# Two-layer hybrid encoder: PSUM banks divided 4 + 2 + 2, third branch's halves interleaved, one address residue for all matmul operands

## The chip, the cores and the metric

One core of a Trainium2 chip. The metric is the device time of one launch in microseconds (us); lower is better. TensorE multiplies, ScalarE (ACT) and VectorE (DVE) and GpSimd (POOL) do the elementwise work, SyncE (SP) issues the transfers.

## The reference

Input x is 256 tokens of 1024 channels, fp32. Two layers, each of three residual steps:

```
x = x + 0.5 * (silu(g) * u) @ w_ffn1_out          # g, u = split(rmsnorm(x) @ w_ffn1_in), 2816 wide each
h = rmsnorm(x); all of q, k, v and the three gates come from one product h @ w_in
a = softmax(rotary(norm(q)) @ rotary(norm(k))) @ v     # 8 heads on 2 key heads
b = softmax(q @ k + bias, window 128, with a sink) @ v # 8 heads on 2 key heads
c = norm((softmax1 - lambda * softmax2) @ v)           # 4 heads, 128 wide
m = sum over i in (a, b, c) of sigmoid(gate_i) * (i @ w_branch[i])   # 512 -> 1024 each
x = x + m @ w_out
x = x + 0.5 * swiglu(rmsnorm(x))                  # ffn2
```

At the end a last rmsnorm. All of it is in fp32.

## The kernel before

Activations stand feature-major: a tile is 128 channels by 256 tokens. A fp32 product is made of three fast ones. Every weight tile (1 MB) is loaded by SP into raw, rounded on ScalarE into hi (L302), and the rest, raw - hi, is made on VectorE as lo (L303); every activation is kept as such a pair too (xgh and xgl, hh and hl, ych and ycl, mh and ml). The helper mm3 issues for one 128x128 block hi with xh (L319), hi with xl (L320), lo with xh (L321), 256 columns each, into the same PSUM bank. hi and lo are split two tiles ahead of use, in three buffers each (pools whi and wlo); split allocates 32 elements more than a tile holds, and for the last FFN's output weights puts the data 16 elements in (L295 to L297). Ahead of everything three pools hold a pad of 16 elements (L112).

PSUM has eight banks of 128 x 512 fp32: four in pool acc under the tag bank (scores sc, transposed probabilities pt, yt, the output accumulators facc of an FFN and wacc of the mixer), one in acc under the tag o (value products o and oc, sums stps), three in wk (gate and up products gu, projections fm, values vps, branch products br). A bank is handed out in rotation and its first writer waits for the last reader of what it held before.

An FFN (ffn, L407) goes over 11 pairs of weight tiles: gate product, up product, then gr = silu on VectorE, ScalarE and POOL, hid = up * gr, the pair hh and hl, and the output product of the previous pair into facc. The last FFN makes its output token-major, with the hidden activations as the stationary operand and hi and lo moving.

The mixer (L618) makes keys, the first queries and values; then a generator (rest) yields projections and branch products in a fixed order (ORDER), and between yields step() takes the next piece of attention from a plan: scores, softmax, transposition, value product (pv, L593), and pair_out (L598 to L602), which reads the bank o and adds the halves into y. branch (L828) makes the products of the first two branches: per half n of the output two wk banks, 48 products; gated (L812) multiplies them with the gates (L817 for the first branch, L820 with an add on POOL, L821, for others). In the first half the k = 3 products come last, since the last y is made late. branch_c (L850) does the third branch: the first half in wk, and behind the sigmoid of its gate (L865) the second half in two banks of acc, three k steps of both first, then the k = 3 products. For the third branch gated also makes the pair mh (L824, ScalarE) and ml (L825, VectorE), four quarters in all, which the output projection takes one after the other, with four accumulators wacc from acc.

The order on TensorE is that of the program; ScalarE and VectorE are ordered by the scheduler for most of it.

Of the kernel before, what the change touches and what calls it, by code (L numbers as in the profile page):

```python
# [17 lines left out]
P = 128  # L18
# [52 lines left out]
def encoder(ctx: ExitStack, tc: tile.TileContext, a, rope, onehot, out):  # L71
# [12 lines left out]
    wk = ctx.enter_context(tc.tile_pool(name="wk", bufs=3, space=bass.MemoryType.PSUM))  # L84
# [17 lines left out]
    def bank_o(name):  # L102

        return acc.tile([P, 2, S], F32, tag="o", name=name, bufs=1)
# [7 lines left out]
    for pool in (p1, pv_, py):  # L112
        pool.tile([P, 16], F32, tag="pad", name="pad", bufs=1)
# [161 lines left out]
    last = {i for i, (_, shape) in enumerate(specs) if shape[0] == 2 and i >= len(specs) - 3 * NPAIR}  # L275
# [15 lines left out]
    def split(n, eng=None):  # L291

        _, shape = specs[len(parts)]
        raw = raws[len(parts)]

        n_el, off = shape[0] * shape[1], 16 if len(parts) in last else 0
        hi, lo = (pool.tile([P, n_el + 32], F32R, tag=t, name=t)[:, off:off + n_el].rearrange("p (a b) -> p a b", a=shape[0]) for pool, t in ((whi, "hi"), (wlo, "lo")))  # L297
        parts.append((hi, lo))
        n = shape[0] // n
        for i in range(0, shape[0], n):  # L300
            h = slice(i, i + n)
            nc.scalar.copy(out=hi[:, h], in_=raw[:, h])  # L302
            (eng or nc.vector).tensor_sub(lo[:, h], raw[:, h], f(hi[:, h]))  # L303
            yield
# [107 lines left out]
    def ffn(gnext, final=False):  # L412
# [60 lines left out]

        pend = None
        for j in range(NPAIR):
            pss = []
            for half in range(2):
                w = weights()
                ps = bank(wk, "gu")
                if j == 0 and half == 0:  # L480
                    project_first(ps, w)
                    stats_tok()
                else:
                    project(ps, w, 0)
                    if j == 0:
                        stats_bcast()
                    project(ps, w, 1)
                pss.append(ps)
            Rb = bc(state["R"], 2)
            gr = t2("gr")  # L490
            nc.vector.tensor_mul(gr, pss[0], Rb)
            nc.scalar.activation(out=gr, in_=gr, func=AF.Silu)  # L492
            nc.gpsimd.tensor_mul(gr, gr, Rb)  # L493
            hid = t2("hid")
            nc.vector.tensor_mul(hid, pss[1], gr)
            hh, hl = t2("hh", F32R), t2("hl", F32R)
            nc.scalar.copy(out=hh, in_=hid)  # L497
            nc.gpsimd.tensor_sub(hl, hid, f(hh))  # L498
            if pend:
                outp(*pend)  # L500
            pend = (j, hh, hl)
            if final and 2 <= j < 4:
                back(j - 2)
            if j == len(late):
                late.append(load_late(j))
# [107 lines left out]
    def mixer(l):  # L613
# [192 lines left out]
        def products(pss, w, y, ks, started):  # L806
            for mp in range(2):
                for t in range(2):
                    for k in ks:
                        mm3(pss[mp][:, t, :], w, k, cs(2 * mp + t), y[0][:, k, :], y[1][:, k, :], False, k == 3, start=(not started and k == 0 and t == 0))  # L810

        def gated(i, n, pss):  # L812
            for mp in range(2):
                m = 4 * n + 2 * mp
                ms, g = (T["gate", b][:, m:m + 2, :] for b in (0, i))
                if i == 0:
                    nc.vector.tensor_mul(ms, pss[mp], g)  # L817
                else:
                    tmp = t2("tmp")
                    nc.vector.tensor_mul(tmp, pss[mp], g)  # L820
                    nc.gpsimd.tensor_add(ms, ms, tmp)  # L821
                if i == 2:
                    mh, ml = t2("mh", F32R), t2("ml", F32R)
                    nc.scalar.copy(out=mh, in_=ms)  # L824
                    nc.vector.tensor_sub(ml, ms, f(mh))  # L825
                    merged.append((mh, ml))

        def branch(i, y, steps):  # L828
# [3 lines left out]
            for n in range(2):  # L832
                w = weights()
                pss = [bank(wk, "br") for _ in range(2)]
                if n == 0:
                    products(pss, w, y, range(3), False)
                    products(pss, w, y, (3,), True)
                else:
                    products(pss, w, y, range(4), False)
                gated(i, n, pss)  # L840
                for _ in range(2):
                    yield

        def branch_c(y, steps):
            while done[0] < steps:
                step()
            w0 = weights()
            ps0 = [bank(wk, "br") for _ in range(2)]
            products(ps0, w0, y, range(3), False)
# [4 lines left out]
            ps1 = [bank(acc, "br") for _ in range(2)]  # L854
            products(ps1, w1, y, range(3), False)
            products(ps0, w0, y, (3,), True)
            gated(2, 0, ps0)
            yield
            products(ps1, w1, y, (3,), True)
            gated(2, 1, ps1)  # L860
# [23 lines left out]
        ps_k = bank(wk, "fm")  # L884
# [26 lines left out]
        vps = [bank(wk, "vps") for _ in range(2)]  # L911
# [137 lines left out]
```

## Time and profile before

| | |
|---|---|
| median of 3 runs | 1228.72 us (1228.0 to 1229.53) |
| profiled execution | 1229.28 us |
| its span | 1227.2 us |
| mean granted TensorE clock | 0.988 |
| TensorE, weight loads, VectorE, ScalarE, POOL busy | 1185.0, 1160.7, 815.9, 677.5, 273.9 us |
| read from HBM | 215.59 MB |

The span runs from the first to the last instruction in the profile. Times in the rows below are microseconds from its start. PE is TensorE, PEld its weight loads, which overlap with products; a product's duration includes its way through the array, so the time from the start of one to the start of the next tells what it costs.

### The profile page before, as it was taken

The numbers are of one execution on the slowest core, as the hardware profiler recorded it, in microseconds if no ns is written. First come the engines' busy times: TensorE is split into PE (matmuls) and PEld (weight loads), VectorE is DVE, ScalarE is ACT, GpSimd is POOL, SyncE is SP. The second block draws the span as 40 slices with busy tenths as digits, with TensorE's granted clock in tenths as the row PEclk, the third lists the DMA queues.
The fourth block names the chain that finished last, engine by engine and source line by source line (L and its number), as shares of the span: only waits on it lengthen the run. The fifth ranks groups of instructions, "written<-read, shape, count | busy, mean of one in ns | idle before, by whom it ended". The sixth has DMA issues, their size and how long they took to land.

```text
span 1227.2 us, 23207 instructions
## 1 busy us (share of the span) xinstructions
PE 1185.0 (97%) x9748; PEld 1160.7 (95%) x9748; DVE 815.9 (66%) x1137; ACT 677.5 (55%) x1117; POOL 273.9 (22%) x196
## 2 busy tenths in 40 slices
PE   8999999998999799999999999999999979999997
PEld 8999999898999699999999999998999969999996
DVE  5755558878886485555575555597887965656564
ACT  6444346579875363444463444466998655444443
POOL 2222214300021142222242222241000222222221
PEclk9999999999999799999999999999999989999999
DMA  7759565454445355555555555555454453655550
GB/s 261 241 180 301 199 199 174 143 172 136 164 155 175 125 186 183 195 188 190 184 194 184 195 189 189 184 161 172 144 159 144 150 183 115 206 177 199 180 200 35
DMA packets 169364, 218.15 MB, mean 178 GB/s; under 512 B 4302, under 2 KB 147200, under 8 KB 169260
## 3 DMA queue, kind: packets, MB, share of 16 engines
q1 hardware_dynamic: 168652, 215.09, 53.2%
q8 instruction: 76, 1.25, 0.4%
q10 hardware_dynamic: 464, 1.06, 0.2%
q0 software_dynamic: 144, 0.52, 0.1%
q14 instruction: 28, 0.23, 0.1%
HBM read 215.59 MB, written 4.22 MB: 179 GB/s over the span
## 4 chain that ended last, share of the span: by engine, by line
PE 77%; ACT 9%; DVE 7%; issue 3%; POOL 2%; DMA 1%; POOLq 0%; SPq 0%; ACTq 0%; DVEq 0%
PE gu L320 13%; PE gu L319 13%; PE gu L321 13%; PE facc L320 5%; PE facc L319 5%; PE facc L321 5%; PE fm L320 3%; PE fm L319 3%; PE fm L321 3%; DVE lo L303 3%; ACT hi L302 2%; ACT e L611 2%; PE br L320 2%; PE br L319 2%; PE br L321 2%
## 5 line engine op out<-in xcount | busy, mean ns | idle before, releaser
L302 ACT CAST hi<-raw 128x1024 fp32r<-128x1024 f32 (+1 forms) x394 | 399.5, 1044 | 412.2 <-issue 368.7
L303 DVE TENSOR_TENSOR lo<-raw,hi 128x1024 fp32r<-128x1024 f32 x390 | 509.7, 1330 | 152.3 <-ACT hi L302 151.6
L321 PE MATMUL gu<-xgh,lo 128*128 128x256 f32 x1408 | 389.9, 277 | 1.9 <-DVE lo L303 1.0
L319 PE MATMUL gu<-xgh,hi 128*128 128x256 f32 x1408 | 391.1, 278 | 0.3 <-ACT hi L302 0.3
L320 PE MATMUL gu<-xgl,hi 128*128 128x256 f32 x1408 | 391.1, 278 | 0.1
L321 PEld LDWEIGHTS gu<-xgh,lo 128*128 128x128 f32 x1408 | 264.3, 188 | 2.5 <-DVE lo L303 1.4
L319 PEld LDWEIGHTS gu<-xgh,hi 128*128 128x128 f32 x1408 | 264.3, 188 | 1.8 <-ACT hi L302 1.3
L320 PEld LDWEIGHTS gu<-xgl,hi 128*128 128x128 f32 x1408 | 264.2, 188 | 1.6 <-DVE xgl L334 0.5
L319 PE MATMUL fm<-xgh,hi 128*128 128x256 f32 x640 | 178.8, 279 | 0.8 <-DVE vc L953 0.8
L320 PE MATMUL fm<-xgl,hi 128*128 128x256 f32 x640 | 178.3, 279 | 0.1
L321 PE MATMUL fm<-xgh,lo 128*128 128x256 f32 x640 | 177.5, 277 | 0.0
L493 POOL TENSOR_TENSOR gr<-gr,R 128x512 f32<-128x512 f32 x44 | 84.3, 1915 | 411.4 <-ACT gr L492 411.4
L320 PE MATMUL facc<-hl,hi 128*128 128x256 f32 x528 | 149.2, 283 | 0.0
L319 PE MATMUL facc<-hh,hi 128*128 128x256 f32 x528 | 147.2, 279 | 0.0
L321 PE MATMUL facc<-hh,lo 128*128 128x256 f32 x528 | 147.1, 279 | 0.0
L319 PEld LDWEIGHTS fm<-xgh,hi 128*128 128x128 f32 x640 | 120.6, 188 | 1.3 <-ACT hi L302 0.7
L320 PEld LDWEIGHTS fm<-xgl,hi 128*128 128x128 f32 x640 | 120.6, 188 | 0.9 <-DVE xgl L334 0.3
L321 PEld LDWEIGHTS fm<-xgh,lo 128*128 128x128 f32 x640 | 120.5, 188 | 0.0
L498 POOL TENSOR_TENSOR hl<-hid,hh 128x512 fp32r<-128x512 f32 x44 | 77.9, 1771 | 104.7 <-ACT hh L497 104.7
L319 PEld LDWEIGHTS facc<-hh,hi 128*128 128x128 f32 x528 | 99.1, 188 | 0.0
L321 PEld LDWEIGHTS facc<-hh,lo 128*128 128x128 f32 x528 | 99.0, 187 | 0.0
L320 PEld LDWEIGHTS facc<-hl,hi 128*128 128x128 f32 x528 | 98.8, 187 | 0.0
(227 smaller groups left out, 1700.0 us busy)
## 6 DMA issues: line engine op xcount, KB each, us to landing
raw<-in_w_ffn_in_dram SPq DMA_DIRECT2D x87, 1024.0 KB, 5.1
raw<-in_w_ffn_out_dram SPq DMA_DIRECT2D x44, 1024.0 KB, 4.9
raw<-in_w_in_dram SPq DMA_DIRECT2D x38, 1024.0 KB, 5.1
raw<-in_w_branch_dram SPq DMA_DIRECT2D x12, 1024.0 KB, 5.1
raw<-in_w_out_dram SPq DMA_DIRECT2D x8, 1024.0 KB, 4.8
G<-skew SPq DMA_DIRECT2D x24, 192.0 KB, 4.6
raw<-in_w_in_dram SPq DMA_DIRECT2D x8, 512.0 KB, 4.5
skew<-vec_d SPq DMA_DIRECT2D x6, 512.0 KB
```

The source lines that it names most:

```text
L302: nc.scalar.copy(out=hi[:, h], in_=raw[:, h])
L303: (eng or nc.vector).tensor_sub(lo[:, h], raw[:, h], f(hi[:, h]))
L319: nc.tensor.matmul(ps, lhsT=hi[:, k, sl], rhs=xh, start=st, stop=False, **chk)
L320: nc.tensor.matmul(ps, lhsT=hi[:, k, sl], rhs=xl, start=False, stop=False, **chk)
L321: nc.tensor.matmul(ps, lhsT=lo[:, k, sl], rhs=xh, start=False, stop=last, **chk)
L493: nc.gpsimd.tensor_mul(gr, gr, Rb)
L498: nc.gpsimd.tensor_sub(hl, hid, f(hh))
L611: nc.scalar.activation(out=e[:, qt, :], in_=e[:, qt, :], func=AF.Identity, scale=su[:, qt:qt + 1])
```

## The change

- PSUM: the four banks of acc stay, the tag o gets two banks, wk two instead of three. The mixer's first projection ps_k and the values vps go from wk to acc; the third branch's second half (ps1) goes from acc to the tag o.
- FFN: the silu of the gate is issued behind the gate product, not behind the up product.
- Branches: products of one bank at a time. In the first half bank 1 begins after three k steps of bank 0, then bank 0's last step, its gating, bank 1's last two steps. In the third branch one bank of the second half is begun before the first half's last steps and the other made whole after them; the two quarters of the second half are merged in reverse.
- The third branch's adds go from POOL to VectorE.
- Addresses: hi and lo lose their 32 extra elements and the offset of 16; three pools get pads of 48, 80 and 48 elements, and the last FFN's hh and hl lie in one tile. In the built program all hi and lo buffers start at residue 384 modulo 512 bytes (in before 384, 0, 128 for hi and 256, 384, 0 for lo); the moving operands xgh, xgl, hh, hl, mh, ml and y at 64 (in before 64 for xgh and xgl, 192 for hh, hl, mh, ml, 320 for y).

```diff
-    wk = ctx.enter_context(tc.tile_pool(name="wk", bufs=3, space=bass.MemoryType.PSUM))
+    wk = ctx.enter_context(tc.tile_pool(name="wk", bufs=2, space=bass.MemoryType.PSUM))
...
-        return acc.tile([P, 2, S], F32, tag="o", name=name, bufs=1)
+        return acc.tile([P, 2, S], F32, tag="o", name=name, bufs=2)
...
-    for pool in (p1, pv_, py):
-        pool.tile([P, 16], F32, tag="pad", name="pad", bufs=1)
+    for pool, n in ((p1, 48), (p4, 80), (py, 48)):
+        pool.tile([P, n], F32, tag="pad", name="pad", bufs=1)
...
-        n_el, off = shape[0] * shape[1], 16 if len(parts) in last else 0
-        hi, lo = (pool.tile([P, n_el + 32], F32R, tag=t, name=t)[:, off:off + n_el].rearrange("p (a b) -> p a b", a=shape[0]) for pool, t in ((whi, "hi"), (wlo, "lo")))
+        hi = whi.tile([P] + shape, F32R, tag="hi", name="hi")
+        lo = wlo.tile([P] + shape, F32R, tag="lo", name="lo")
...
+        def silu(ps):
+            Rb = bc(state["R"], 2)
+            gr = t2("gr")
+            nc.vector.tensor_mul(gr, ps, Rb)
+            nc.scalar.activation(out=gr, in_=gr, func=AF.Silu)
+            nc.gpsimd.tensor_mul(gr, gr, Rb)
+            return gr
...
+                project(ps, w, 0)
+                project(ps, w, 1)
+                gr = silu(ps)
+            w, pu = weights(), bank(wk, "gu")
+            project(pu, w, 0)
...
+            if final:
+                hp = t4("hp")
+                hh, hl = hp[:, 0], hp[:, 1]
...
+        def products(ps, w, y, mp, ks):
+            for t in range(2):
+                for k in ks:
+                    mm3(ps[:, t, :], w, k, cs(2 * mp + t), y[0][:, k, :], y[1][:, k, :], False, k == 3, start=(k == 0 and t == 0))
...
+                (nc.gpsimd if i == 1 else nc.vector).tensor_add(ms, ms, tmp)
...
+                    products(ps[0], w, y, 0, (0, 1, 2))
+                    products(ps[1], w, y, 1, (0, 1))
+                    products(ps[0], w, y, 0, (3,))
+                    gated(i, n, 0, ps[0])
+                    products(ps[1], w, y, 1, (2, 3))
+                    gated(i, n, 1, ps[1])
...
-            ps1 = [bank(acc, "br") for _ in range(2)]
-            products(ps1, w1, y, range(3), False)
-            products(ps0, w0, y, (3,), True)
-            gated(2, 0, ps0)
+            ps1 = [bank_o("br") for _ in range(2)]
+            products(ps1[0], w1, y, 0, range(3))
+            for mp in range(2):
+                products(ps[mp], w, y, mp, (3,))
+                gated(2, 0, mp, ps[mp])
             yield
-            products(ps1, w1, y, (3,), True)
-            gated(2, 1, ps1)
+            products(ps1[1], w1, y, 1, range(4))
+            gated(2, 1, 1, ps1[1])
+            products(ps1[0], w1, y, 0, (3,))
+            gated(2, 1, 0, ps1[0])
+            merged[2:] = merged[:1:-1]
...
-        ps_k = bank(wk, "fm")
+        ps_k = bank(acc, "fm")
...
-        vps = [bank(wk, "vps") for _ in range(2)]
+        vps = [bank(acc, "vps") for _ in range(2)]
```

What moves on TensorE, at the end of the first layer's third branch. First the order before, from the transposition yt to the end of the branch (br_4770 and br_4771 are the two banks of the first half, br_4816 and br_4817 those of the second; one row stands for the start of each run of products):

```order
L693 MATMUL yt_4808<-ident_96,of_4727 128x128 x2
L319 MATMUL br_4816<-ych_3861,hi_4682 128x256
...
L319 MATMUL br_4817<-ych_3861,hi_4682 128x256
...
L319 MATMUL br_4770<-ych_3861,hi_4624 128x256
...
L319 MATMUL br_4771<-ych_3861,hi_4624 128x256
...
L319 MATMUL br_4816<-ych_3861,hi_4682 128x256
...
L319 MATMUL br_4817<-ych_3861,hi_4682 128x256
...
L319 MATMUL wacc_4906<-mh_4869,hi_4764 128x256
```

Now:

```order
L699 MATMUL yt_4808<-ident_96,of_4727 128x128 x2
L317 MATMUL br_4816<-ych_3861,hi_4682 128x256
...
L317 MATMUL br_4770<-ych_3861,hi_4624 128x256
...
L317 MATMUL br_4771<-ych_3861,hi_4624 128x256
...
L317 MATMUL br_4817<-ych_3861,hi_4682 128x256
...
L317 MATMUL br_4816<-ych_3861,hi_4682 128x256
...
L317 MATMUL wacc_4906<-mh_4845,hi_4764 128x256
```

Before, 18 products of br_4816 and 18 of br_4817 stand ahead of the first half's last k step (6 products of each bank), and 6 and 6 behind it. Now 18 of br_4816 stand ahead, and br_4817 follows whole, 24 products, with br_4816's last 6 at the end.

On VectorE, the same place, from the last ycl on. Before (tmp is the gated product, ml the low part of a merged quarter, lo a half of a weight tile's split):

```order
L697 SCALAR_TENSOR_TENSOR ycl_3862<-yt_4808,sub_134,ych_3861 128x256
L820 TENSOR_TENSOR tmp_4866<-br_4770,gates2_4439 128x512
L303 TENSOR_TENSOR lo_4913<-raw_4680,hi_4912 128x1024
L825 TENSOR_TENSOR ml_4870<-gates0_2814,mh_4869 128x512
L820 TENSOR_TENSOR tmp_4873<-br_4771,gates2_4439 128x512
L303 TENSOR_TENSOR lo_4913<-raw_4680,hi_4912 128x1024
L303 TENSOR_TENSOR lo_4919<-raw_4762,hi_4918 128x1024
L825 TENSOR_TENSOR ml_4877<-gates0_2814,mh_4876 128x512
L820 TENSOR_TENSOR tmp_4892<-br_4816,gates2_4439 128x512
```

Now:

```order
L703 SCALAR_TENSOR_TENSOR ycl_3862<-yt_4808,sub_134,ych_3861 128x256
L824 TENSOR_TENSOR tmp_4842<-br_4770,gates2_4439 128x512
L825 TENSOR_TENSOR gates0_2814<-gates0_2814,tmp_4842 128x512
L301 TENSOR_TENSOR lo_4913<-raw_4680,hi_4912 128x1024
L829 TENSOR_TENSOR ml_4846<-gates0_2814,mh_4845 128x512
L824 TENSOR_TENSOR tmp_4855<-br_4771,gates2_4439 128x512
L301 TENSOR_TENSOR lo_4913<-raw_4680,hi_4912 128x1024
L825 TENSOR_TENSOR gates0_2814<-gates0_2814,tmp_4855 128x512
L301 TENSOR_TENSOR lo_4919<-raw_4762,hi_4918 128x1024
L829 TENSOR_TENSOR ml_4859<-gates0_2814,mh_4858 128x512
L824 TENSOR_TENSOR tmp_4886<-br_4817,gates2_4439 128x512
L301 TENSOR_TENSOR lo_4919<-raw_4762,hi_4918 128x1024
```

Behind each tmp now comes the add into gates0, which POOL made; the halves of the lo splits are now spread one by one between tmp, add and ml.

## Rows read from the trace of the kernel before

**Rows 1.** The page: span, and busy time by engine (share of the span, instructions).

```profile
span 1227.2 us, 23207 instructions
...
PE 1185.0 (97%) x9748; PEld 1160.7 (95%) x9748; DVE 815.9 (66%) x1137; ACT 677.5 (55%) x1117; POOL 273.9 (22%) x196
```

**Rows 2.** Waits of TensorE: line, releaser, us in all, times, longest.

```profile
PE wacc L319 <- DVE tmp L820: 15.2, 4, 4.4
...
PE o L593 <- DVE y L601: 4.6, 4, 1.4
...
PE o L593 <- ACT e L611: 3.5, 2, 1.8
...
PE o L593 <- ACT es L646: 1.4, 1, 1.4
```

**Rows 3.** Timeline of TensorE, mixer's end: start, us, instruction, idle before and its releaser.

```profile
398.39 0.28 PE L321 MATMUL br<-ych,lo 128*128 128x256 f32 x1
...
399.43 0.38 PE L319 MATMUL wacc<-mh,hi 128*128 128x256 f32 x1 [0.76 <-ACT mh L824]
...
405.69 0.55 PE L319 MATMUL wacc<-mh,hi 128*128 128x256 f32 x1 [4.38 <-DVE tmp L820]
...
433.40 0.28 PE L319 MATMUL gu<-xgh,hi 128*128 128x256 f32 x1
...
1000.61 0.28 PE L321 MATMUL br<-ych,lo 128*128 128x256 f32 x1
...
1034.98 0.28 PE L319 MATMUL gu<-xgh,hi 128*128 128x256 f32 x1
```

**Rows 4.** Timeline of ScalarE and VectorE, end of the third branch.

```profile
392.85 1.92 ACT L865 ACTIVATE gates<-gates 128x2048 f32<-128x2048 f32 x1
...
395.16 0.48 DVE L697 SCALAR_TENSOR_TENSOR ycl<-yt,sub,ych 128x256 fp32r<-128x256 f32 x1 [2.18 <-ACT ych L696]
...
399.73 0.68 DVE L825 TENSOR_TENSOR ml<-gates,mh 128x512 fp32r<-128x512 f32 x1
...
404.87 0.68 DVE L820 TENSOR_TENSOR tmp<-br,gates 128x512 f32<-128x512 f32 x1
```

**Rows 5.** Windows: busy time by engine, granted clock (PEclk), DMA.

```profile
290.00:300.00 10.00, 8.61 (x76) 8.45 (x75) 9.63 (x27) 9.88 (x26) 0.74 (x1) 1.00 0.45 146
...
410.00:420.00 10.00, 10.00 (x65) 10.00 (x66) 2.39 (x3) 2.62 (x3) 1.20 (x1) 0.72 0.12 42
```

**Rows 6.** Timeline of TensorE, first instruction of weight tiles in two FFNs.

```profile
40.40 0.28 PE L319 MATMUL gu<-xgh,hi 128*128 128x256 f32 x1
...
46.10 0.28 PE L319 MATMUL gu<-xgh,hi 128*128 128x256 f32 x1
...
51.54 0.28 PE L319 MATMUL facc<-hh,hi 128*128 128x256 f32 x1
...
57.24 0.28 PE L319 MATMUL gu<-xgh,hi 128*128 128x256 f32 x1
...
457.00 0.28 PE L319 MATMUL facc<-hh,hi 128*128 128x256 f32 x1
...
462.70 0.28 PE L319 MATMUL gu<-xgh,hi 128*128 128x256 f32 x1
...
473.59 0.28 PE L319 MATMUL facc<-hh,hi 128*128 128x256 f32 x1
```

**Rows 7.** Timeline of TensorE and VectorE, first and second branch products.

```profile
341.62 0.28 PE L319 MATMUL br<-yah,hi 128*128 128x256 f32 x1
...
349.69 0.28 PE L319 MATMUL br<-ybh,hi 128*128 128x256 f32 x1
...
341.79 1.29 DVE L817 TENSOR_TENSOR gates<-br,gates 128x512 f32<-128x512 f32 x2 [0.93 <-ACT gates L865]
...
349.83 2.35 DVE L303 TENSOR_TENSOR lo<-raw,hi 128x1024 fp32r<-128x1024 f32 x2
...
352.10 0.68 DVE L817 TENSOR_TENSOR gates<-br,gates 128x512 f32<-128x512 f32 x1
```

More of the change, by code (lines that the diff above doesn't have):

```diff
@@ L274, in encoder @@
         specs += ffn_chunks(a["w_ffn2_in"][l], a["w_ffn2_out"][l])
-    last = {i for i, (_, shape) in enumerate(specs) if shape[0] == 2 and i >= len(specs) - 3 * NPAIR}
     specs[0] = ([((slice(None), slice(2 * i, 2 * i + 2)), specs[0][0][0][1][:, 2 * i:2 * i + 2]) for i in range(4)],) + specs[0][1:]
@@ L472, in outp @@
                 kouter(accs, weights(j < NPAIR - 1), hh, hl, j == 0, j == NPAIR - 1, evac)
+        def silu(ps):
[5 more added lines that the diff above has]
+            return gr
         pend = None
         for j in range(NPAIR):
[L476 to L493, printed above, removed]
-            hid = t2("hid")
-            nc.vector.tensor_mul(hid, pss[1], gr)
-            hh, hl = t2("hh", F32R), t2("hl", F32R)
+            w, ps = weights(), bank(wk, "gu")
+            if j == 0:
+                project_first(ps, w)
+                stats_tok()
+            else:
+                project(ps, w, 0)
[3 more added lines that the diff above has]
+            project(pu, w, 0)
+            if j == 0:
+                stats_bcast()
+                gr = silu(ps)
+            project(pu, w, 1)
+            hid = t2("hid")
+            nc.vector.tensor_mul(hid, pu, gr)
+            if final:
+                hp = t4("hp")
+                hh, hl = hp[:, 0], hp[:, 1]
+            else:
+                hh, hl = t2("hh", F32R), t2("hl", F32R)
             nc.scalar.copy(out=hh, in_=hid)
@@ L804, in mixer, with gated @@
         merged = []
[L806 to L826, printed above, removed]
+        def products(ps, w, y, mp, ks):
+            for t in range(2):
+                for k in ks:
+                    mm3(ps[:, t, :], w, k, cs(2 * mp + t), y[0][:, k, :], y[1][:, k, :], False, k == 3, start=(k == 0 and t == 0))
+        def gated(i, n, mp, ps):
+            m = 4 * n + 2 * mp
+            ms, g = (T["gate", b][:, m:m + 2, :] for b in (0, i))
+            if i == 0:
+                nc.vector.tensor_mul(ms, ps, g)
+            else:
+                tmp = t2("tmp")
+                nc.vector.tensor_mul(tmp, ps, g)
+                (nc.gpsimd if i == 1 else nc.vector).tensor_add(ms, ms, tmp)
+            if i == 2:
+                mh, ml = t2("mh", F32R), t2("ml", F32R)
+                nc.scalar.copy(out=mh, in_=ms)
+                nc.vector.tensor_sub(ml, ms, f(mh))
+                merged.append((mh, ml))
         def branch(i, y, steps):
@@ L833, in branch @@
                 w = weights()
-                pss = [bank(wk, "br") for _ in range(2)]
+                ps = [bank(wk, "br") for _ in range(2)]
                 if n == 0:
-                    products(pss, w, y, range(3), False)
-                    products(pss, w, y, (3,), True)
-                else:
[L839 to L842, printed above, removed]
+                    products(ps[0], w, y, 0, (0, 1, 2))
[4 more added lines that the diff above has]
+                    gated(i, n, 1, ps[1])
+                    yield
+                else:
+                    for mp in range(2):
+                        products(ps[mp], w, y, mp, range(4))
+                        gated(i, n, mp, ps[mp])
+                        if mp == 0:
+                            yield
+                yield
         def branch_c(y, steps):
@@ L846, in branch_c @@
                 step()
-            w0 = weights()
-            ps0 = [bank(wk, "br") for _ in range(2)]
-            products(ps0, w0, y, range(3), False)
+            w = weights()
+            ps = [bank(wk, "br") for _ in range(2)]
+            for mp in range(2):
+                products(ps[mp], w, y, mp, range(3))
             while done[0] < len(plan):
@@ L853, in branch_c @@
             w1 = weights(False)
-            ps1 = [bank(acc, "br") for _ in range(2)]
-            products(ps1, w1, y, range(3), False)
-            products(ps0, w0, y, (3,), True)
-            gated(2, 0, ps0)
-            yield
-            products(ps1, w1, y, (3,), True)
-            gated(2, 1, ps1)
+            ps1 = [bank_o("br") for _ in range(2)]
+            products(ps1[0], w1, y, 0, range(3))
+            for mp in range(2):
+                products(ps[mp], w, y, mp, (3,))
+                gated(2, 0, mp, ps[mp])
+            yield
+            products(ps1[1], w1, y, 1, range(4))
[3 more added lines that the diff above has]
+            merged[2:] = merged[:1:-1]
             yield
```

## The prediction

> **What bounds the kernel now.** I read the page's busy table first: TensorE is busy for 1185.0 of 1227.2 us [rows 1]. So a gain must come from the 42 us in which it stands idle, or from matmuls that take longer than they need. The profiled execution took 1229.28 us, 2.1 more than its span, and 0.56 above the median 1228.72; the sum below is made against 1229.28. A difference under 0.2% (2.5 us) I count as none.
>
> The view of waits by TensorE line names the idle time [rows 2]. The largest entry is the output projection (wacc) waiting for tmp, the product with the third branch's gates: 15.2 us in 4 waits. Next are the value products (o), which wait on VectorE and ScalarE work on an earlier pair: 4.6, 3.5 and 1.4, so 9.5 us.
>
> The timeline of TensorE between the last branch product and the next FFN shows what the first entry is worth [rows 3]. In layer 0 the last branch product starts at 398.39, the first wacc at 399.43; the third wacc bank opens at 405.69 after 4.38 us of waiting, and the next FFN starts at 433.40. VectorE reads the bank that wacc wants (tmp, 404.87, 0.68 us) [rows 4]: the bank is one of the two that hold the branch's second half in the pool that wacc also draws from. The granted clock of the window 410 to 420 is 0.72 [rows 5], so after the waits part of the matmuls ran at the lower level of 1.2 GHz.
>
> Last, the pitch. The 48 matmuls that use one weight tile in an FFN (a gate, an up or an output product) should take equally long everywhere. In the first FFN gate, up and output products run from 40.40 to 46.10, 51.54 and 57.24: 5.70, 5.44 and 5.70 us. In the second, an output runs from 457.00 to 462.70, and gate and up from there to 473.59: 5.70, and 10.89 for two [rows 6]. Same shape, same clock, no wait: 113.3 against 118.8 ns a matmul. In the first FFN ten gates and ten outputs are slow; in each of the next two FFNs all eleven outputs (42 in all, like those rows), and some seven shorter pieces of projections and branches. What goes with it is the address modulo 512 bytes. The three weight buffers have residues 384, 0 and 128 for hi (256, 384 and 0 for lo), since each has 128 bytes of padding; the moving operand has 64 (xgh, xgl) or 192 (hh, hl). The fast group from 46.10 reads hi at 384, so its moving operand is 192 off (64 - 384, modulo 512); its slow neighbours are 64 off. In the second FFN the slow output is 320 off, and the gate and up, at 448 and 64, are fast. So a distance of 64 is found slow in one FFN and fast in the other, while 192 is fast wherever it occurs, even right behind a slow group.
>
> **The change, term by term.**
>
> *A. End of the mixer.* The 192 wacc matmuls need 192 x 113.3 ns = 21.8 us. They take from 398.50 to 433.40 (34.9) and from 1000.72 to 1034.98 (34.3) [rows 3]: 13.1 and 12.5 us lost, waits and low clock together. With the second half's banks out of wacc's pool, no wacc bank waits for tmp. In exchange only 18 products, not 36, stand before the last k step of the first half, so 18 x 0.1133 = 2.0 us of cover goes: in before those 36 end at 395.78 and the last ycl at 395.64 [rows 4], so TensorE will wait about 2.0 us there in each layer, behind the sigmoid (392.85, 1.92 us). After it come 42 products (4.8 us), and wacc can start at 400.5. Is its input there? VectorE: tmp 0.68, add (which POOL did, taken like ml) 0.68, a lo split of 1.2 between, ml 0.68; with ScalarE's mh the first quarter is ready at about 400.3. The others take about 4.3 us each (tmp, add, ml and two lo): 404.6, 408.9, 413.2, against needs at 400.5, 405.9, 411.4, 416.8. So wacc runs through. A = -(13.1 + 12.5) + 2 x 2.0 = **-21.6**. Bounds: -25.6 if the sigmoid wait is covered, -17 if each of the eight quarters comes about half a microsecond late.
>
> *B. Second o bank.* 9.5 us of waits [rows 2]; a pair no longer waits for the previous pair's sums to be read. Not all will go: in 290 to 300 ScalarE is busy 9.88 of 10 us [rows 5], and it makes the next pair's probabilities. I take **-7**; bounds 0 (only the name of the wait changes) and -11 (waits and the clock they cost).
>
> *C. Two projection banks, not three.* New waits where a branch opens its third and later banks. The first branch's second chunk starts at 341.62, while the first gated product, which frees a bank, runs from 341.79 (pair 1.29) [rows 7]: 0.9 us. The second branch's next bank is wanted at 349.69 (plus that 0.9), and the gated product that frees it is at 352.10 to 352.78, behind two lo splits from 349.83 on: 2.2 us. So 3.1 us per layer, and layer 1 has the same order: **+6**. Bounds: +1 (the products issued earlier let VectorE read sooner) and +10 (it delays scores too, and ScalarE has no slack).
> In the FFNs two banks do: gate's bank is read by gr while up runs (5.44 us), up's by hid while output and the next gate run. The silu issued earlier is hidden by up. Cost 0; without that cover a gr and a hid, 0.69 us each as tmp, would stand in each of 44 pairs. ps_k and vps in the four-bank pool are read before the first scores need it: 0.
>
> *D. Addresses.* In the changed kernel all hi and lo have one residue, 384, and all moving operands of the projections 64, so the distance is 192, for hi and lo alike (in before lo is 320 off where hi is 192), for gate, up, projections, branches, wacc, and the first three FFNs' outputs. That is the distance always fast in before. 42 x 0.26 us = 10.9, and the shorter pieces 1.1: **-12**. It is 0 for the last FFN's output, whose pitch I leave as it is; if it rose by the same 5.70 to 5.44, its 11 tiles would cost 11 x 0.26 = 2.9. Bounds for D: -13 and 0 (it doesn't matter); +35 is a rival.
> The Trainium skill speaks against this term: SBUF — State Buffer, section Who interferes with whom, gives TensorE one read port for the moving operand and an independent one for the weights, and says that it never waits on anyone. By it addresses make no difference and the sum would be 12 us smaller. The 5.70 and 5.44 of rows 6 don't agree with it, since no wait lies inside either group.
>
> Adds from POOL to VectorE: four per layer, on the chain of A, counted there. Transfers, their bytes and queue order stay: 0.
>
> Sum: -21.6 - 7 + 6 - 12 = -34.6, so 1229.28 - 34.6 = 1194.7, or 1194.1 against the median. I forecast **1194 us**.
>
> **Rivals.**
> 1. *Addresses don't matter.* For it: the 118.8 ns might come with what else runs. Against it: the same line is fast and slow by tile. D = 0: 1206. Chance 0.12. The port rule of the Trainium skill's page SBUF — State Buffer, section Who interferes with whom, would give this time.
> 2. *VectorE's order becomes the bound.* lo splits stand ahead of add and ml in its in-order queue; the second to fourth quarter come late, as 4.38 us did, and the clock falls again. Half of A stays: 1194 + 11 = 1205. For: today's wait behind tmp at 404.87 came after two lo splits. Against: 1.3 us or more of slack at each. Chance 0.10.
> 3. *The second o bank gives nothing,* because ScalarE is full there: B = 0, 1201. Chance 0.10.
> 4. *Slower: the uniform distance is the slow state.* The state of a group depends on more than its own distance, since 64 is found in both, and lo's distance is new; with all buffers alike the alternation that brings the fast groups might be gone. 4224 gate and up, 1920 projection, 1584 output, 384 wacc and 576 branch products are 181 groups; some 134 are fast now. Slow, they cost 134 x 0.26 = +35 in place of -12: 1194 + 47 = 1241. It decides the sign from 87 slow groups on (the other terms' 22.6 us by 0.26). Against: in before that distance is fast right behind slow groups. Chance 0.05.
>
> **How the numbers follow.** The forecast has 0.63: its own range from the terms' bounds is 1187 to 1201. Rivals 1 to 3 are all faster; together with the forecast 0.95. To hold 8 in 10 the range reaches from 1185 to 1207. Chance of faster 0.94, same 0.01, slower 0.05. The range leaves out the slow rival and the ends where two rivals meet.
>
> **What would show it.** In the changed profile: no wacc wait on tmp, one of about 2 us before the third branch's last k step, next FFN about 11 us sooner after the branch and no window of clock 0.7 there; o waits under 3 us; new waits of br on the gated product, 1 and 2 us; every 48-matmul group of the first three FFNs 5.44 us. The forecast is wrong if the busy time of TensorE stays while only waits change (rival 1), if wacc still waits for VectorE (rival 2), or if groups of 5.70 us are everywhere (rival 4).

## The result, and the profile after

The changed kernel takes 1215.14 us (median of 4 runs, 1213.06 to 1218.68) against 1228.36 of the kernel before: a ratio of 0.9894, interval 0.9869 to 0.9919. So it is faster, by 13 us (1.1%). The forecast was 34, its range ended at 1207, and the time lies outside it. The profiled execution took 1213.06 us.

The page of the changed kernel, beside [rows 1]:

```profile
span 1211.2 us, 23246 instructions
...
PE 1179.2 (97%) x9748; PEld 1155.5 (95%) x9748; DVE 854.2 (71%) x1145; ACT 678.3 (56%) x1117; POOL 251.1 (21%) x188
```

TensorE's busy time fell by only 5.8 us, the idle time by 10. The view of waits by TensorE line, beside [rows 2]:

```profile
PE br L317 <- DVE gates L808: 7.2, 2, 3.6
...
PE gu L317 <- DVE gr L475: 2.3, 1, 2.3
...
PE br L317 <- DVE gates L821: 2.2, 2, 1.2
...
PE gu L317 <- ACT xt L427: 1.6, 2, 0.8
...
PE wacc L317 <- ACT mh L828: 1.0, 2, 0.5
...
PE wacc L318 <- DVE ml L829: 0.7, 2, 0.3
```

The 15.2 us of wacc behind tmp are gone, as forecast, and so are all waits of the value products. New are 7.2 us in which branch products wait for VectorE's read of the last gate projection (gates, L808), 2.2 for the first branch's gated product (L821), 1.5 in which scores wait for ScalarE's kas, and in the FFNs 2.3 behind gr and 1.6 behind xt, ScalarE's copy of the last FFN's transposed output.

The end of the mixer in the timeline of TensorE, beside [rows 3]:

```profile
401.05 0.28 PE L317 MATMUL wacc<-mh,hi 128*128 128x256 f32 x1
...
424.59 0.28 PE L317 MATMUL gu<-xgh,hi 128*128 128x256 f32 x1
...
991.78 0.28 PE L317 MATMUL wacc<-mh,hi 128*128 128x256 f32 x1
...
1015.32 0.28 PE L317 MATMUL gu<-xgh,hi 128*128 128x256 f32 x1
```

wacc takes 23.54 us in both layers (401.05 to 424.59, 991.78 to 1015.32), where it took 33.97 and 33.27 from its first matmul on. The prediction worked out 21.8 without any wait. The first wacc matmul of the second layer in the kernel before:

```profile
1001.71 0.38 PE L319 MATMUL wacc<-mh,hi 128*128 128x256 f32 x1 [0.83 <-ACT mh L824]
```

Stage by stage, from the first matmul of a stage to that of the next in the timeline of each profiled execution (us; the last stage ends with its last matmul):

| | first FFN | mixer 0 | wacc 0 | two FFNs | mixer 1 | wacc 1 | last FFN |
|---|---|---|---|---|---|---|---|
| before | 190.0 | 200.6 | 34.0 | 368.4 | 199.9 | 33.3 | 184.2 |
| changed | 186.8 | 205.0 | 23.5 | 362.6 | 204.6 | 23.5 | 187.9 |
| old_addr: banks and order alone | 193.4 | 204.4 | 23.4 | 368.6 | 205.0 | 23.4 | 186.3 |
| addr_only: addresses alone | 186.8 | 201.7 | 34.2 | 362.7 | 200.6 | 34.8 | 186.6 |
| after_lo256: 4 + 2 + 2 | 186.6 | 204.5 | 23.2 | 362.8 | 204.7 | 23.2 | 186.5 |
| one_o_lo: 4 + 1 + 2 | 188.2 | 204.2 | 22.1 | 362.9 | 204.6 | 22.1 | 186.4 |
| lo_256: 4 + 1 + 3 | 184.2 | 204.2 | 22.1 | 362.6 | 202.3 | 22.1 | 184.2 |

The table shows where the missing time went. Both mixers got longer by over 4 us and the last FFN by 3.7, where the sum had left them as they were.

In the mixers, waits are the smaller part of it. Windows over the two mixers, of the kernel before and then of the changed one (columns as in [rows 5]; TensorE's busy time is the first number behind the comma, the granted clock the third from the end):

```profile
198.82:399.43 200.61, 192.44 (x1607) 188.47 (x1605) 165.34 (x315) 152.16 (x318) 34.75 (x30) 1.00 0.49 159
801.82:1001.71 199.89, 193.54 (x1607) 189.55 (x1605) 165.10 (x311) 151.51 (x316) 34.51 (x31) 0.99 0.48 159
```

```profile
196.09:401.05 204.96, 196.82 (x1607) 192.66 (x1605) 168.84 (x318) 153.53 (x318) 32.49 (x29) 0.98 0.47 156
787.17:991.78 204.61, 197.10 (x1606) 192.94 (x1605) 168.86 (x315) 153.09 (x317) 32.45 (x30) 0.98 0.47 155
```

For the same matmuls TensorE is busy 7.9 us longer, and idle only 1.1 us longer. Most of that is clock. Steps of 0.19 to 0.26 us from one 256-column matmul to the next, with no wait between, are 138 in the two mixers now and 81 before; at some 0.1 us each the 57 more are an estimated 5.8 us. One such stretch stands right behind the 3.61 us in which the first branch waits (until 333.85):

```profile
334.00:339.00 5.00, 5.00 (x31) 5.00 (x32) 0.99 (x2) 4.97 (x4) 0.00 (x0) 0.66 0.00 0
```

The granted clock is 0.66 there, so TensorE is at the lower of its two levels, 1.2 GHz, for most of it; the kernel before has 1.00 in this window and 47 matmuls in place of 31.

### The profile page after: what moved, and what is told of

Read it like the earlier page. It is cut to its first block, busy times and chain, and to the rows that moved or that the text cites. A ratio compares the mean times of both kernels' runs of the same rounds, so it can differ in the third digit from the quotient of the medians.

```text
span 1211.2 us, 23246 instructions
## 1 busy us (share of the span) xinstructions
PE 1179.2 (97%) x9748; PEld 1155.5 (95%) x9748; DVE 854.2 (71%) x1145; ACT 678.3 (56%) x1117; POOL 251.1 (21%) x188
## 5 line engine op out<-in xcount | busy, mean ns | idle before, releaser
L301 DVE TENSOR_TENSOR lo<-raw,hi 128x1024 fp32r<-128x1024 f32 x390 | 539.4, 1397 | 135.3 <-ACT hi L300 134.5
L300 ACT CAST hi<-raw 128x1024 fp32r<-128x1024 f32 (+1 forms) x394 | 404.0, 1043 | 411.4 <-issue 369.8
L477 POOL TENSOR_TENSOR gr<-gr,R 128x512 f32<-128x512 f32 x44 | 76.9, 1747 | 368.9 <-ACT gr L476 368.9
L318 PE MATMUL facc<-hl,hi 128*128 128x256 f32 x528 | 145.7, 276 | 0.0
L475 DVE TENSOR_TENSOR gr<-gu,R 128x512 f32<-128x512 f32 x44 | 30.4, 691 | 76.9 <-PE gu L319 76.7
```

The costliest lines, as they stand in the source:

```text
L318: nc.tensor.matmul(ps, lhsT=hi[:, k, sl], rhs=xl, start=False, stop=False, **chk)
L475: nc.vector.tensor_mul(gr, ps, Rb)
```

## The experiments

Times are medians; ratios are to the kernel before, run on the same chip, with their 95% intervals.

**The changed kernel again.** 

> The changed kernel once more, for its spread (1213.1 to 1218.7 so far, against 1227.7 to 1229.5 before). Theory: the pitch of the matmuls has two states that an execution falls into, so a second profile shows other weight tiles at 5.54 us in place of 5.33 (first to last of 48 starts), and its time goes with their number, 0.21 us each. Rival: the spread comes from waits; then the same tiles are slow and the idle time differs.

1214.5, ratio 0.9889 (0.9876 to 0.9903), runs from 1214.2 to 1215.1. One half-tile of the changed kernel, first and last of its 24 matmuls, in the first profile and then in the second:

```profile
249.85 0.28 PE L317 MATMUL fm<-xgh,hi 128*128 128x256 f32 x1
...
252.56 0.28 PE L319 MATMUL fm<-xgh,lo 128*128 128x256 f32 x1
```

```profile
250.28 0.29 PE L317 MATMUL fm<-xgh,hi 128*128 128x256 f32 x1
...
252.90 0.28 PE L319 MATMUL fm<-xgh,lo 128*128 128x256 f32 x1
```

2.71 us and 2.62: the same instructions at the same addresses, the long pitch (the time from one start to the next) in one execution and the short one in the other. Of the 181 groups of 48 matmuls, 59 have a median step over 115.5 ns in the first profile and 46 in the second, and 19 changed sides. So the pitch isn't fixed by the program at these addresses. It does not explain the whole spread: the first FFN differs by 1.7 us (186.8 and 188.5) with one long group in either. That difference is clock: the granted clock of 26 to 30 is 1.00 in the first profile and 0.59 in the second, with 18 matmuls in that window in place of 35.

**The two halves of the change.** The kernel before with the new addresses (hi and lo without padding, the pads of 48, 80 and 48, one tile for the last hh and hl), and the changed kernel with the old ones.

```diff
-    for pool in (p1, pv_, py):
-        pool.tile([P, 16], F32, tag="pad", name="pad", bufs=1)
+    for pool, n in ((p1, 48), (p4, 80), (py, 48)):
+        pool.tile([P, n], F32, tag="pad", name="pad", bufs=1)
...
+        hi = whi.tile([P] + shape, F32R, tag="hi", name="hi")
+        lo = wlo.tile([P] + shape, F32R, tag="lo", name="lo")
```

> The kernel before with the change's addresses alone. The prediction's term D says -12 us (1216.5). From the changed kernel's profile, stage by stage: first FFN -5.2, the two middle FFNs -5.8 together, last FFN +3, mixers +1: about -7, so 1221.5, with gate and up of the last FFN slow. Rival (addresses don't matter): 1228.4.

> The changed kernel with the addresses of before. If the two parts add up and the addresses gave 7 us, 1222 (1215 + 7), with ten gates and ten outputs of the first FFN at 5.59 us again, and less spread than the changed kernel, about 2 us. If D was 12 as predicted, 1227. If addresses don't matter, 1215.

addr_only 1223.4, ratio 0.9962 (0.9949 to 0.9975); old_addr 1223.3, ratio 0.9958 (0.9946 to 0.9971). So the addresses give 5 us alone and 9 on top of the new banks, and banks and order alone give 5, where the prediction had 12 for addresses and 22.6 for the rest. Rival 1 falls: addresses matter.

**Banks 4 + 1 + 3.** One value bank, three projection banks; the third branch's second half comes from the latter, its second bank after the first half is gated.

```diff
-    wk = ctx.enter_context(tc.tile_pool(name="wk", bufs=2, space=bass.MemoryType.PSUM))
+    wk = ctx.enter_context(tc.tile_pool(name="wk", bufs=3, space=bass.MemoryType.PSUM))
...
-        return acc.tile([P, 2, S], F32, tag="o", name=name, bufs=2)
+        return acc.tile([P, 2, S], F32, tag="o", name=name, bufs=1)
...
-            ps1 = [bank_o("br") for _ in range(2)]
+            ps1 = [bank(wk, "br")]
...
+            ps1.append(bank(wk, "br"))
             products(ps1[1], w1, y, 1, range(4))
```

> The changed kernel with banks 4 + 1 + 3: one bank for value products, three for projections, the third branch's second half drawn from the latter. Theory (the branch's wait of 3.6 us and the second branch's 1.2 come from the third bank that is gone, and the value products' waits of before were worth less than these): wacc still takes 23.5 us, the branch waits, the 2.3 of gr and the 1.6 of xt go, value waits of some 9 us come back: 1209 to 1212. Rival (ScalarE and VectorE set the pace of the mixer's attention, whatever the banks): mixers stay at 205 us from first projection to wacc, only names of waits change, and 4 us come from the FFNs: 1211 with mixers at 205. Second rival (the second bank for value products was worth its 7): 1218.

1202.7, ratio 0.9794 (0.978 to 0.9807): better than any theory said, 12 us below the changed kernel. In the profile the mixers shrink by 2.2 us each, wacc by 1.1 each, the last FFN by 1.7. The long branch waits and those for gr and xt are gone.

**4 + 1 + 2, a bank unused.** The second value bank taken away without giving the projections a third; the edit of banks_413 with wk left at two and the first of the third branch's last banks from tag o:

```diff
-        return acc.tile([P, 2, S], F32, tag="o", name=name, bufs=2)
+        return acc.tile([P, 2, S], F32, tag="o", name=name, bufs=1)
...
-            ps1 = [bank_o("br") for _ in range(2)]
+            ps1 = [bank_o("br")]
...
+            ps1.append(bank(wk, "br"))
```

> The changed kernel with one bank for value products (4 + 1 + 2, a bank left unused; the second of the third branch's last two banks is drawn from the projections'). It tells the worth of the second value bank apart from that of the third projection bank. If the second value bank was worth the 7 us that the prediction gave it, 1221; if it was worth what its waits of before show and no more than 2 per layer, 1217 to 1219; if it is worth nothing (the pace of the attention is set by ScalarE), 1214.5, with as much waiting on value products as is lost elsewhere.

1211.7, ratio 0.9858 (0.9843 to 0.9873), 3 us below the changed kernel. Beside two projection banks, the second value bank gives nothing; if anything, it costs.

**Distances.** All on 4 + 1 + 3. lo 128 bytes lower by a pad of 96 elements in wlo (the pads of p4 and py drop out, with them the last FFN's stationary operand moves to 64); or hi and lo together at another residue, by a pad in whi (u64, u320, u448; the last two drop the pads of p4 and py too).

```diff
-    for pool, n in ((p1, 48), (p4, 80), (py, 48)):
+    for pool, n in ((wlo, 96), (p1, 80)):
...
+    for pool, n in ((whi, 32), (p1, 16), (p4, 80), (py, 48)):
...
+    for pool, n in ((whi, 96), (p1, 80)):
...
+    for pool, n in ((whi, 64), (p1, 112)):
```

> The 4 + 1 + 3 kernel with lo 128 bytes lower, at 256, so that moving operands lie 192 from hi and 320 from lo, the pair of distances that was always fast in the kernel before; the last FFN's stationary operand moves to 64 with it. Theory (a pair of distances has its own state, and 192 with 320 is free of the slow one): no weight tile at 5.5 us or more in any FFN or projection, 10 us of pitch gone, 1193. Rival (the state is set by what ran before, not by distance): slow tiles stay somewhere, 1198 to 1203.

> The 4 + 1 + 3 kernel with hi and lo at residue 0, so that every moving operand is 64 off. In before this distance was found fast and slow. If a uniform distance is as good as any other, the same tiles as in the 4 + 1 + 3 kernel are slow and the time is 1203; if 192 is better than others, more slow tiles, up to 35 us.

> The same with hi and lo at 256: every moving operand 320 off, which was slow in all outputs of the middle FFNs before (hi 320, lo 448). If distance matters, 5.70 us a tile nearly everywhere and 1230 or more; if what ran before decides, about 1203.

> The 4 + 1 + 3 kernel with hi and lo at 128: every moving operand 448 off, which was found fast in the middle FFNs of the kernel before (hi 448, lo 64). 64 and 320 were slow throughout (1226 and 1224). If slow goes with 64 and 320 alone, no slow tiles and 1200; if any uniform distance but 192 is slow, 1225.

lo_256: 1200.3, ratio 0.9764 (0.9748 to 0.9781). One group of 181 is long, where banks_413 has 68; the first FFN takes 184.2 in place of 186.8 and the last 184.2 in place of 186.2. Of the 10 us that were expected 2.4 came: the mixers, where 30 of the 68 were, did not shrink. u64 took 1226.2, u320 1224.3, u448 1201.6, one run each. u64, the starts of an up, an output and a gate product in the first FFN's timeline:

```profile
30.41 0.28 PE L317 MATMUL gu<-xgh,hi 128*128 128x256 f32 x1
...
36.07 0.28 PE L317 MATMUL facc<-hh,hi 128*128 128x256 f32 x1
...
41.72 0.28 PE L317 MATMUL gu<-xgh,hi 128*128 128x256 f32 x1
```

5.66 and 5.65, and so in every FFN tile of u64 and u320 but the last FFN's outputs (512 columns). TensorE's waits are no longer in these runs than in banks_413, so the 22 to 24 us above it are put down to pitch. By groups of 48, all 181 are long in u64, 162 in u320 (the other 19 stand in the mixers), 40 in u448 and 1 in lo_256. So 64 and 320 for all give the long pitch nearly everywhere, 192 for all gives either, 192 for hi with 320 for lo the short one, and 448 the short one mostly. These runs move the weights alone, so the weights' own residue changed with the distance, and they don't tell the two apart. For the distance speaks that in before hi at 384 was fast with a moving operand at 64 and slow with one at 192 (rows 6 with the prediction's residues).

**The changed banks at the good addresses.** 

> The changed kernel (4 + 2 + 2) with lo at 256 and the last FFN's stationary operand at 64, as in the run lo_256. The shortfall of D is laid to the one residue for lo as well as hi, which leaves the pitch in two states. Then slow tiles go (61 to 69 pieces in two profiles of the changed kernel), some 6 to 8 us: 1207. If the slow tiles come from the banks' order and not from the residue of lo, 1214.

1211.3, ratio 0.9862 (0.9847 to 0.9877): 3 us for the tiles, not 6 to 8. The long ones went (2 groups are left), but the mixers stayed at 204.5 and 204.7: TensorE's idle time there grew instead, to 18.2 us in both from 15.7.

**Value bank, with the pitch out of the way.** 

> The run one_o (4 + 1 + 2) with lo at 256, so that the pitch can't cloud the comparison; beside after_lo256 (4 + 2 + 2, 1211.3) it gives the worth of the second value bank alone. If that bank is worth nothing, as one_o says, 1206 to 1211, with mixers within a microsecond of 204.6; if one_o was only lucky in its pitch, 1214 or more.

1208.7, ratio 0.9835 (0.982 to 0.985). Waits of after_lo256 (two value banks), then of one_o_lo (one):

```profile
PE br L317 <- DVE gates L808: 7.7, 2, 3.9
...
PE br L317 <- DVE gates L821: 2.4, 2, 1.2
```

```profile
PE o L599 <- DVE y L607: 4.1, 3, 1.4
...
PE br L317 <- DVE gates L821: 3.9, 2, 1.9
...
PE o L599 <- ACT e L617: 3.2, 2, 1.8
...
PE o L599 <- ACT es L652: 2.8, 2, 1.4
```

With one value bank 10.1 us of value waits come and the 7.7 on the gates' read shrink to 0.8; the mixers are equal within 0.3 us. The shorter waits also spare the clock at this place. The window 325 to 350, with the granted clock behind the busy times, of after_lo256 and then of one_o_lo:

```profile
325.00:350.00 25.00, 20.39 (x161) 19.99 (x159) 18.65 (x43) 19.92 (x34) 1.47 (x2) 0.93 0.42 143
```

```profile
325.00:350.00 25.00, 23.36 (x200) 22.79 (x198) 19.39 (x44) 20.93 (x36) 1.48 (x2) 1.00 0.44 144
```

And of lo_256 (4 + 1 + 3), for the same lines and the third branch:

```profile
PE o L599 <- ACT e L617: 3.6, 2, 1.8
...
PE o L599 <- DVE y L607: 3.3, 3, 1.3
...
PE br L317 <- ACT ych L702: 3.1, 2, 1.5
...
PE o L599 <- ACT es L652: 1.3, 1, 1.3
```

With a third projection bank the branches wait for no gated product any more; the value waits stay, 8.2 us of them. 1208.7 to 1200.3 is the price of that bank, 8.4 us; by the stages 4.0 in the first FFN (the wait for gr is 2.1 of it), 2.3 in mixer 1 and 2.2 in the last FFN (xt, 1.6). Some of it is clock that comes and goes between executions: some 1.5 of the first FFN's 4.0 is a stretch at a granted clock of 0.58 (26 to 30 in one_o_lo) like that in the changed kernel's second profile.

**What sets the pace of the attention.** The division of probabilities by their sums is left out (so the result lacks it): 0.91 us of ScalarE for each of 16 heads of a layer, and with it the reciprocal of the sums, 0.16 us of VectorE. Both stand in the chain from scores to value product.

```diff
-            normalize(e, su)
```

> The changed kernel with the division of the first two branches' probabilities by their sums left out: on ScalarE two activations less for each of 16 heads of a layer, 0.91 us a head, and a small reciprocal on VectorE. Theory (ScalarE, through VectorE's queue, sets the pace of the attention; the second value bank only moved the wait to the branch): the branch's wait of 3.6 us on the gates' read shrinks to under 1, mixers from 204.7 to about 200 us, 1204 in all. Rival (VectorE alone or the two projection banks as such set it): mixers stay within 1 us, 1213.

> The run one_o (4 + 1 + 2 banks) with the same division left out, to tell what the second value bank is worth once ScalarE has time. Theory: now the value products wait for their bank with ScalarE free, so the second bank is worth something: this stays 3 to 7 us above nonorm_422. Rival (the second bank is worth nothing whatever ScalarE does): equal, or below it as with the division (1211.7 against 1214.5).

nonorm_422 1205.9 (0.982, 0.9805 to 0.9835); mixers 201.5 and 202.0. nonorm_412 1216.0 (0.9893, 0.9876 to 0.9909), with mixers 201.6 and 203.2. So both mixers shrink without the division. The wait for the gates' read fell from 7.2 to 4.0 us in nonorm_422, not to under 1 each as expected (the longest is 2.3). The 10 us between the two runs are elsewhere. Two starts in one of the middle FFNs, of nonorm_422 at the short pitch and then of nonorm_412 at the long one:

```profile
467.86 0.28 PE L317 MATMUL gu<-xgh,hi 128*128 128x256 f32 x1
...
473.30 0.28 PE L317 MATMUL gu<-xgh,hi 128*128 128x256 f32 x1
```

```profile
467.52 0.28 PE L317 MATMUL gu<-xgh,hi 128*128 128x256 f32 x1
...
473.17 0.28 PE L317 MATMUL gu<-xgh,hi 128*128 128x256 f32 x1
```

5.44 us a tile against 5.65, with the same distances; the two middle FFNs took 362.8 and 375.8 us, and 65 of their 66 groups are long in the second. With lo at 256, which leaves the short pitch:

> The run nonorm_422 (division left out, 4 + 2 + 2) with lo at 256: mixers near 201.5 again, no slow tiles, 1200 to 1203.

> The run nonorm_412 (division left out, 4 + 1 + 2) with lo at 256. In nonorm_412 the two middle FFNs took 375.8 us in place of 362.7, so its 10 us above nonorm_422 are pitch. If the second value bank is worth nothing even with ScalarE relieved, this equals nonorm_422_lo within 2 us or is below it; if it is worth something then, 3 us or more above it.

1203.0 (0.9787, 0.9773 to 0.9802) and 1203.1 (0.9788, 0.9771 to 0.9804). Equal: with two projection banks the second value bank is worth nothing even then. Beside after_lo256 and one_o_lo, with the division, the mixers are 3 to 4 us shorter each (200.4 to 201.9 against 204.2 to 204.7).

**VectorE relieved.** Half of each mixer weight tile's lo split on POOL.

```diff
+        mix = 3 * NPAIR <= len(parts) % (len(specs) // DEPTH) < len(specs) // DEPTH - 3 * NPAIR
...
-            (eng or nc.vector).tensor_sub(lo[:, h], raw[:, h], f(hi[:, h]))
+            (eng or (nc.gpsimd if mix and i else nc.vector)).tensor_sub(lo[:, h], raw[:, h], f(hi[:, h]))
```

> The run lo_256 (4 + 1 + 3) with half of each mixer weight tile's lo split on POOL in place of VectorE. If VectorE sets the pace of the attention, value waits and mixers shrink, 2 us or more per layer: 1196. If it's ScalarE, unchanged at 1200; if POOL's longer instructions come into the attention's own chain, 1202 or more.

1239.4, ratio 1.0082 (1.0058 to 1.0106), 39 us slower than lo_256. The costliest group on POOL, and a wait:

```profile
L302 POOL TENSOR_TENSOR lo<-raw,hi 128x1024 fp32r<-128x1024 f32 x64 | 163.7, 2559 | 173.5 <-ACT hi L301 143.6 <-PE sc L577 15.8 <-DVE ml L830 4.6
...
PE o L600 <- DVE y L608: 13.4, 6, 4.5
```

A split takes 2.56 us on POOL, and VectorE is held up while it runs. One of POOL's splits in the timeline, and an add of VectorE on two columns beside it:

```profile
314.97 3.07 POOL L302 TENSOR_TENSOR lo<-raw,hi 128x1024 fp32r<-128x1024 f32 x1 [0.28 <-ACT hi L301]
...
316.05 2.01 DVE L654 TENSOR_TENSOR su<-su,es 128x2 f32<-128x2 f32 x1 [0.26 <-ACT es L653]
```

That add takes at most 0.161 us in all its 16 places in lo_256. Here it ends at 318.06, when POOL's split ends (318.04). VectorE's products qc (L529, 64x512) take 1.27 us on average in place of 0.69. So this doesn't tell what VectorE's share in the pace is.

**Two smaller parts**, on lo_256: the adds back on POOL, the silu late.

```diff
-                (nc.gpsimd if i == 1 else nc.vector).tensor_add(ms, ms, tmp)
+                nc.gpsimd.tensor_add(ms, ms, tmp)
...
-                gr = silu(ps)
             project(pu, w, 1)
+            gr = silu(ps)
```

> The run lo_256 (1200.3) with the third branch's adds back on POOL. If the move to VectorE is what lets wacc run through (POOL's add takes about twice as long, and each quarter waits for it), wacc takes 2 us more per layer: 1204. If the new banks and order alone did it, 1200; less if VectorE's queue was the tighter one.

> The run lo_256 with silu issued behind the up product, as in the kernel before. Costed at nothing in the prediction, since up's product hides it: 1200. If the early silu matters for the two or three banks of the FFN, slower by up to 0.69 us in each of 44 pairs.

pool_add 1202.5 (0.9787, 0.977 to 0.9803), 2 us above lo_256, intervals overlapping; wacc 22.5 and 23.6 in place of 22.1. late_silu 1199.2 (0.9763, 0.9748 to 0.9777): no difference.

## Why the prediction was wrong

- *Term A* held. wacc lost 10.4 and 9.7 us; I had 12.2 and 11.5 for that stage. What is left above 21.8 is 1.7 us a layer: waits of the first quarter for mh and ml (1.7 in both layers together) and some long tiles. Rival 2, later quarters held up by VectorE's order, did not come. The 2 us of sigmoid wait that I charged did not show: TensorE came to its 18 covering products later, 0.55 us behind the start of the sigmoid (393.99 and 393.44). In lo_256 it came 1.5 before it (386.43 and 387.95), and the wait is there (ych, 3.1 in two).
- *Term B* failed: -7 for the second value bank, measured 0 (without the division) to +3 (one_o against the changed kernel; +2.6 with lo at 256). Rival 3's number, at a chance of 0.10, was the case. The step that failed is "a pair no longer waits for the previous pair's sums": true, but TensorE then meets the same lateness at its next wait. The branch's start shows it. Before, first branch product and the read of the last gate projection that precedes it:

```profile
333.84 0.28 PE L319 MATMUL br<-yah,hi 128*128 128x256 f32 x1
...
335.75 0.69 DVE L802 TENSOR_TENSOR gates<-fm,R 128x512 f32<-128x512 f32 x1
```

Now, with ScalarE's copy of y and VectorE's queue up to that read:

```profile
327.95 0.28 PE L317 MATMUL br<-yah,hi 128*128 128x256 f32 x1
...
330.06 0.36 ACT L605 COPY y<-o 64x256 f32<-64x256 f32 x1
...
331.36 0.42 DVE L607 TENSOR_TENSOR y<-y,o 64x256 f32<-64x256 f32 x1
...
331.81 0.69 DVE L586 TENSOR_TENSOR ptl<-pt,pth 128x512 fp32r<-128x512 f32 x1
...
332.42 0.41 DVE L641 CUSTOM_DVE_ANT_0 e<-sc,G 128x256 f32<-128x256 f32 x1
...
333.11 0.69 DVE L808 TENSOR_TENSOR gates<-fm,R 128x512 f32<-128x512 f32 x1
...
333.85 0.39 PE L317 MATMUL br<-yah,hi 128*128 128x256 f32 x1 [3.61 <-DVE gates L808]
```

TensorE comes to the branch 5.9 us earlier (327.95, not 333.84), the read only 2.6 (333.11, not 335.75). Of both, 2.7 us is the earlier start of the mixer (196.09, not 198.82): counted from there TensorE comes 3.2 us earlier, and the read no earlier at all (137.0 us behind the start, 136.9 before). It stands in VectorE's order behind the sums of y, which wait for ScalarE, and behind the attention's next steps. The one long wait also cost clock, which the sum had at nothing for B and C: 0.66 in 334 to 339, above. I saw 9.88 of 10 us of ScalarE [rows 5] and took a quarter off for it; all of it had to go. That the division has a part in that lateness is shown by the runs without it, 3 to 4 us a mixer. Most of it is ScalarE's work, but its time in the chain and VectorE's reciprocal went too, so ScalarE's and VectorE's shares stay open. Open too is whether a second value bank is worth something beside three projection banks: every run that has it has two, and the wait that it met is for one of these.
- *Term C* was mis-sized and incomplete: +6, measured 8.4 (one_o_lo to lo_256), some of it clock. The 0.9 us at the first branch's second chunk was not what came; the bank that is missing there is that of the last gate projection, wanted already by the second of the first branch's banks (3.61 us). I counted banks among branches and left out the projection in front. The 2.2 us at the second branch came as 1.2. And "in the FFNs two banks do" is wrong at both ends: gr in the first tile pair waits for the norm's factor (2.3), the last FFN's transpositions take the banks too (1.6).
- *Term D*: -12, measured -8.8 (old_addr to changed). The three FFNs that had long tiles before gave 6.6 (the first) and 6.0 (the two in the middle); of the 6.6 some 1.6 is clock, 0.60 in 26 to 30 of old_addr. But the step "192, the distance always fast in before" took hi's distance for the whole; there lo stood at 320. With both at 192 a tile takes either time, and the last FFN, whose gates and ups were short before, got long ones (16 of their 22 groups, before 1): 187.9 us, not 184.2. With lo at 256 they are short again and it takes 186.5 (after_lo256), so 1.4 of the 3.7 goes with the addresses. Part of rival 4 was true: in one execution, that of nonorm_412, the two middle FFNs ran at the long pitch nearly throughout. The short pitch that I had seen comes with lo at 256.
- By the stages of the profiled executions: wacc stays 3.5 us above the sum, the mixers are 9.1 longer where the sum left them as they were (sigmoid, B, C and D against each other), mostly by the lower clock, first and last FFN lie 5.7 above it. That is 18.3 of the 18.4 us by which the profiled execution falls short of 34.6; its own 2.1 below the median is the rest.

Of the Trainium skill, SBUF — State Buffer, section Who interferes with whom, the runs say that its rule that TensorE never waits on anyone does not cover this case: 22 to 24 us hang on where its own two operands lie modulo 512 bytes (u64 and u320 against banks_413, one run each).

## What to carry to other kernels

A wait that is removed is worth nothing where the engine that ends it stays as late as it was: look how long after the wait's end that engine is busy, and where the next wait for it stands. A long wait can cost clock besides: behind 3.6 us of waiting the granted clock here was 0.66. Count every user of a bank pool around a place, the producer in front included. A pattern that is always fast must be kept whole (both operands' distances, not one), and one profile doesn't show whether a pitch is the same in every execution: take a second.

The version that beats both is 4 + 1 + 3 banks with lo at 256 (lo_256): 1200.3 us, 28 below before, 14 below the change.

## What the runs showed of the hardware

Matmuls of 256 columns cost 113.3 or some 118 ns with nothing else changed but where the operands lie modulo 512 bytes. In the changed kernel, two starts in the first FFN (output and gate) and two in the last (gate and up):

```profile
36.99 0.28 PE L317 MATMUL facc<-hh,hi 128*128 128x256 f32 x1
...
42.43 0.28 PE L317 MATMUL gu<-xgh,hi 128*128 128x256 f32 x1
...
1131.04 0.28 PE L317 MATMUL gu<-xgh,hi 128*128 128x256 f32 x1
...
1136.69 0.28 PE L317 MATMUL gu<-xgh,hi 128*128 128x256 f32 x1
```

5.44 us a tile in the first, 5.65 in the last, all at a distance of 192. With that distance for hi and lo alike the pitch changes between executions and holds for long stretches; I have no run that shows what sets it. Distances of 64 and 320 for all gave the long pitch (one run each; in u320 not in 19 groups of the mixers), 192 with 320 the short one, each over some thousand matmuls. Whether the distance alone decides, or the residues of both operands, is not shown.

A long instruction of POOL can hold a short one of VectorE: in lo_pool an add on 128x2 elements took 2.01 us beside a split on POOL, and at most 0.161 in lo_256.
